# Delta rule in a two-layer trunk: the 32x32 blocks of all chunks inverted by one substitution on VectorE, operands kept in DRAM, weights split once for both halves

## Chip, cores and metric

One core of a Trainium2 chip runs the whole program. The metric is the device time of one execution in microseconds, given as the median of several runs. The profile is one more execution with the hardware profiler on.

## Reference

A trunk of two layers over 1024 tokens of width 1024, all in float32. Layer 0 mixes tokens with a spatial gate (GMLP) and a gated delta rule; layer 1 with differential attention. Each layer then has an MLP and a gated per-layer embedding. Only the delta rule of layer 0 and what shares its input projection matter here:

```
proj = rms_norm(h) @ w_in                     # 1024 x 3080
u, v, q, k, v', z, beta_logit, a_logit = split(proj)
a_out = gelu(u) * (tril(w_s) @ layer_norm(gelu(v)) + b_s)      # per group, 128 tokens at a time
q, k, v' = silu(causal_conv4(q, k, v'));  q, k normalised per head
g = -exp(a_log) * softplus(a_logit + dt_bias);  beta = sigmoid(beta_logit)
# gated delta rule, 4 heads of 128, chunk by chunk:
gc    = cumsum(g);  decay = exp(gc_i - gc_j), lower triangle
A     = strict_lower((beta * k) @ k^T * decay)
T     = inverse(I + A)                        # unit lower triangular
v_new = T @ (beta * v') - T @ (beta * k * exp(gc)) @ state
o     = (q * exp(gc)) @ state + ((q @ k^T) * decay) @ v_new
state = state * exp(gc_last) + (k * exp(gc_last - gc))^T @ v_new
b_out = rms_norm(o) * silu(z)
h     = h + concat(a_out, b_out) @ w_out
```

The reference uses chunks of 64 tokens; the kernel uses 8 chunks of 128, which gives the same result.

## The kernel before

`trunk` runs `even_mix` (layer 0's mixing), then the MLP, embedding and attention. The sequence is held in two halves of 512 tokens. A float32 product is made from three single-pass matmuls (`mm3`: hi x hi, hi x lo, lo x hi). A weight tile is loaded raw (`Weight.load`), cast to its hi part on ScalarE and its lo part taken on VectorE (`split`, lines 220 and 221). Eight raw pieces and twelve split tiles are held.

In `even_mix` two streams share the engines. The first, called fill, is a generator over all tiles of the input projection followed by the first half of the output product (`mix_first`). One step of it, a unit, is three or six matmuls, one or two rows of an output tile's sum. `pump(n)` advances the fill until n units are issued. Each projection tile is 256 columns wide. In the version before, q, k and v of each half are separate tiles (`proj_qkv(i, hf)`), z is shared by the halves (`proj_z`), and u and v of the gate are again separate by half (`proj_uv(hf)`): 22 tiles, each with four split pieces. A q, k or v tile is followed on VectorE by the convolution (L1203, L1209, L1212), and the gate's parts by a layer norm (`norm_v`), small products (`gate`, pgm) and transposes (`put_a`, `put_b`, pab).

The second stream is the recurrence. Per chunk it has three generators. `prep(c)` makes the two decay matrices from pd (L1359, masked at L1360), k's transposes and lengths (pk, L1368 to L1373), the matrix am of k products (pkk, L1394), and the scaled v, q and q-k products (pv, pq, pkq). `inverse(c)` inverts I + A. It takes the sixteen 32x32 diagonal blocks (4 heads, 4 blocks; L1426), inverts them by doubling in four rounds, each with a masked copy on GpSimd (L1434), 16 small products into py, a copy on ScalarE (L1441), 16 into pz, a subtraction (L1449) and a transpose (L1451) on VectorE, and then joins blocks to 64 and to 128 with four more products. Each small float32 product shows as two instructions in the profile. `step(c)` advances the state (pks, po, pvn, pst), and `emit_out` normalises the chunk's output.

The order of issue is written out by hand. A chunk has 12 slots; `chunk` says which generator advances in which slot (`FRONT`), and `FILLS` how many units of fill are issued in it. The recurrence is issued at high priority (`EARLY`). A fill matmul may not come before the recurrence's last matmul of `LAG` = 3 slots earlier (`Ordered`). All instructions go through a scheduler that orders them by a simulated time line before the program is built.

Tiles named by a tag (`slot("c6", ...)`) have one place for each tag; a new tile with the tag waits for the old one's readers.

Of the kernel before, what the change touches and what calls it, by code (L numbers as in the profile page):

```python
# [29 lines left out]
FRONT = (5, 6, 8, 9, 11)  # L30
# [4 lines left out]
FILL0 = (9, 10, 7, 10)  # L35
FILLS = ((0, 2, 1, 4, 5, 4, 0, 1, 3, 1, 4, 1), (0, 3, 2, 3, 1, 5, 3, 1, 4, 0, 3, 0), (0, 6, 2, 2, 2, 3, 0, 1, 3, 0, 3, 2), (0, 5, 3, 5, 4, 6, 1, 2, 5, 1, 4, 2), (0, 7, 5, 4, 0, 8, 0, 0, 7, 0, 3, 3), (1, 6, 3, 3, 5, 2, 1, 2, 5, 2, 3, 1), (1, 5, 0, 3, 2, 4, 3, 2, 4, 1, 5, 6), (0, 3, 5, 6, 6, 3, 4, 3, 3, 2, 4, 1), (1, 0, 1, 1, 0, 4, 0, 1, 0, 2, 3, 0))
# [77 lines left out]
class Trunk:  # L114
# [969 lines left out]
    def even_mix(self, first, rows_of_rest, rest_of_x, w_in, ws, bs, conv, a_log, dt_bias, v_gain, o_gain, masks, w_out, gain_next, h_dram):  # L1084
# [90 lines left out]
        qkv = {}  # L1175

        def proj_qkv(i, hf):
            return [proj_qkv_tile(i, hf, j) for j in range(2)]

        def proj_qkv_tile(i, hf, j):  # L1180
            def units(w):
                if j == 0:
                    qkv[i, hf] = self.slot(f"A{i + 3 * hf}", [P, G, HT], F32, "qkv")

                first = (i, hf, j) == (1, 0, 0)
                pss = [self.mm_ps() for _ in range(2)] if first else []
                for k, ml in itertools.product(range(KT), range(2)) if first else ():
                    self.mm3(pss[ml], w.at(k, slice(ml * P, (ml + 1) * P)), hs_first[k], k == 0, k == KT - 1)
                    if k < KT - 1:
                        yield None  # L1190
                for ml in range(2):
                    m = i * 4 + j * 2 + ml
                    ps = pss[ml] if first else self.mm_ps()
                    for k in range(0 if first else KT):
                        self.mm3(ps, w.at(k, slice(ml * P, (ml + 1) * P)), hs[hf][k], k == 0, k == KT - 1)
                        if k < KT - 1:
                            yield None
                    cx = self.slot(f"c{10 + m % 2}", [P, 3 + HT], F32, "cx")
                    if hf:
                        nc.vector.tensor_copy(cx[:, 0:3], tails[:, m])  # L1200
                    else:
                        nc.vector.memset(cx[:, 0:3], 0.0)
                    nc.vector.tensor_tensor(cx[:, 3:], ps, rb[hf], ALU.mult)  # L1203
                    if not hf:
                        nc.vector.tensor_copy(tails[:, m], cx[:, HT : HT + 3])
                    y = self.tmp()
                    nc.scalar.activation(y, cx[:, 3:], AF.Copy, scale=conv[:, 3, m : m + 1])
                    for tap in range(3):
                        nc.vector.scalar_tensor_tensor(y, cx[:, tap : tap + HT], conv[:, tap, m : m + 1], y, ALU.mult, ALU.add)  # L1209
                    th = self.tmp()  # L1210
                    nc.scalar.activation(th, y, AF.Tanh, scale=0.5)
                    nc.vector.scalar_tensor_tensor(qkv[i, hf][:, m % 4], th, 1.0, y, ALU.add, ALU.mult)  # L1212
                    yield None

            c0 = 1024 + i * 512 + j * 256
            return Proj(f"qkv{hf}", [(w_in[:, c0 : c0 + 256], 0)], 256, units, 16, qkv_lo)


# [16 lines left out]
        def proj_z(j):  # L1235
            def units(w):
                for t2 in range(4):
# [12 lines left out]
                    yield from proj_tok("z", w, t2, done)  # L1250

# [5 lines left out]
        def proj_uv(hf):  # L1257
            g = {}

            def tile_(col, j):  # L1260
                def units(w):
                    if j == 0:
                        g[col] = self.slot((("A1", "A2"), ("A2", "A0"))[col > 0][hf], [P, 4, 512], F32, "guv")
                    for t2 in range(2):
                        def done(ps):
                            for i in range(2):
                                nc.scalar.activation(g[col][:, 2 * t2 + i, j * 256 : (j + 1) * 256], ps[i], AF.Gelu_apprx_tanh, scale=rt(4 * hf + 2 * t2 + i))
                            if j == 1:
                                if col:
                                    norm_v(t2)  # L1270
                                else:
                                    gate(t2)

                        yield from proj_tok(f"uv{hf}", w, 2 * hf + t2, done)
                    if j == 1 and col == 0:
                        yield from put_a()
                        if hf == 0:
                            yield from put_b(0)

                c0 = col + j * 256  # L1280
                return Proj(f"uv{hf}", [(w_in[:, c0 : c0 + 256], 0)], 256, units, 16, uv_lo)

            def norm_v(t2):
                gv = g[512]
                if t2 == 0:
                    g["vg"] = self.slot("c10", [P, 512], F32, "vg")
                    nc.sync.dma_start(g["vg"], v_gain.partition_broadcast(P))
# [14 lines left out]
                for i in range(2):  # L1302
                    t = 2 * t2 + i
                    x = gv[:, t].rearrange("p (g d) -> p g d", d=HD)
                    nc.vector.tensor_tensor(x, x, bc(rv[:, 4 * i : 4 * i + 4], HD), ALU.mult)
                    nc.gpsimd.tensor_tensor(gv[:, t], gv[:, t], g["vg"], ALU.mult)

            def gate(t2):
                gv, gu = g[512], g[0]
                for t in (2 * t2, 2 * t2 + 1):  # L1310
                    ps = aux([P, G, HD], "aux", "pgm")
                    for i in range(G):
                        self.pe.matmul(ps[:, i], lhsT=wT[:, i], rhs=gv[:, t, i * HD : (i + 1) * HD], start=True, stop=True)
                    for i in range(G):
                        a = gu[:, t, i * HD : (i + 1) * HD]
                        nc.vector.scalar_tensor_tensor(a, ps[:, i], bs[:, i : i + 1], a, ALU.add, ALU.mult)

            def put_a():
                for i in range(G):
                    pt = aux([P, 4, P], "tr", "pab")  # L1320
                    for t in range(4):
                        self.pe.transpose(pt[:, t], g[0][:, t, i * HD : (i + 1) * HD], self.ident)
                    put_ab(hf, i, pt)
                    yield

            return [tile_(col, j) for col in (512, 0) for j in range(2)]
# [8 lines left out]
        def put_b(hf):  # L1335
            assert not hf or not outs
            for i in range(G):
                pt = aux([P, 4, P], "tr", "pab")
# [6 lines left out]
        ch = {}  # L1345

        def prep(c):
            hf, cs = c // 4, slice((c % 4) * P, (c % 4 + 1) * P)


# [5 lines left out]
            for own, other in ((gsum, 1), (nsum, -1)):  # L1356
# [5 lines left out]
                yield  # L1362
            dl, du = out
            q, k, v = (qkv[i, hf][:, :, cs] for i in range(3))

            def inverse_length(pt, name):
                sq = self.slot(f"c{4 + c % 2}", [P, G, HD], F32, "sq")
                nc.scalar.activation(sq, pt, AF.Square)  # L1368
                l2 = self.sp.tile([P, G], F32, tag="l2", name=self.nm("l2"))
                nc.vector.tensor_reduce(l2, sq, AX.X, ALU.add)  # L1370
                nc.vector.tensor_scalar(l2, l2, 4 * EPS, None, ALU.add)
                rn = self.sp.tile([P, G], F32, tag=name, name=self.nm(name), bufs=3)
                nc.gpsimd.tensor_tensor(rn, l2, self.mhalf[:, 0:G], ALU.pow)  # L1373
                return rn
# [5 lines left out]
            nc.vector.tensor_tensor(kt, pt, bc(dec[:, c], HD), ALU.mult)  # L1380
            rk = inverse_length(pt, "rk")

            sc = self.sp.tile([P, 3, G], F32, tag="sc", name=self.nm("sc"), bufs=3)
            nc.vector.tensor_tensor(sc[:, 0], rk, rk, ALU.mult)
            nc.vector.tensor_tensor(sc[:, 0], sc[:, 0], beta[:, c], ALU.mult)
            nc.vector.scalar_tensor_tensor(sc[:, 1], sc[:, 0], -1.0, ec[:, c], ALU.mult, ALU.mult)
# [217 lines left out]
        def chunk(st, inv, front, n):  # L1604
            for i in range(12):
                if i in (0, 2, 4):
                    run(st)
# [153 lines left out]
```

## Time and profile before

| | before |
|---|---|
| median of 3 runs | 2600.97 us (2600.1 to 2601.56) |
| profiled execution | 2601.79 us, its span 2600.1 us |
| instructions | 45173 |
| TensorE clock, mean | 0.999 |
| HBM read, written | 277.60 MB, 93.85 MB |
| VectorE busy | 1856.7 us |

`even_mix` takes about the first 500 us of the span: the first projection matmul starts at 10 us, the recurrence's first products at about 84 us, and the last chunk's product po at 452 us. The busy columns of the profile are unions of intervals. The matmul ends are modelled, so a group's mean of one instruction is longer than the distance from one to the next. In a group line the part after the bar is busy time and the mean of one in ns; after the second bar stands the engine's idle time just before these instructions, and what ended it.

### The profile page before, as it was taken

What the parts mean: (1) busy time and instruction counts of PE and PEld (TensorE: products, weight loads), DVE (VectorE), ACT (ScalarE), POOL (GpSimd) and SP (SyncE); (2) the same over time, 40 slices, a digit from 0 to 9 for tenths busy, and PEclk for the clock granted to TensorE, in tenths of its full rate; (3) what the DMA queues carried; (4) which work ended last, traced back from release to release, by engine and by line L of the source; (5) the groups of instructions that cost most, each with busy time, mean ns of one, the idle gap of its engine ahead of it and who ended that gap; (6) DMA issues with size and microseconds to landing.
All of it is one profiled execution on the core that took longest, in us unless ns stands there. A gap on an engine that the chain in (4) does not pass through costs nothing.

```text
span 2600.1 us, 45173 instructions
## 1 busy us (share of the span) xinstructions
PE 2571.4 (99%) x16606; PEld 2212.6 (85%) x16606; DVE 1856.7 (71%) x3736; ACT 1282.0 (49%) x2528; POOL 301.6 (12%) x288
## 2 busy tenths in 40 slices
PE   9999999999999999999999999999999999999999
PEld 7878989888888887888899999988778888888899
DVE  7788667678767779656567777786887677787542
ACT  6543443455445444444446666655654555445421
POOL 0212423000000000000234334310000000000000
PEclk9999999999999999999999999999999999999999
DMA  7322222536555865553311111136466558655511
GB/s 245 86 54 55 75 62 92 166 126 226 196 177 185 282 206 186 188 181 118 109 41 60 42 42 58 62 114 228 167 217 206 170 184 282 207 185 192 185 58 45
DMA packets 281237, 374.42 MB, mean 144 GB/s; under 512 B 25300, under 2 KB 163256, under 8 KB 281016
## 3 DMA queue, kind: packets, MB, share of 16 engines
q1 hardware_dynamic: 280568, 371.47, 43.8%
q8 instruction: 130, 2.13, 0.3%
q14 instruction: 91, 0.75, 0.1%
q10 hardware_dynamic: 448, 0.07, 0.0%
HBM read 277.60 MB, written 93.85 MB: 143 GB/s over the span
## 4 chain that ended last, share of the span: by engine, by line
PE 94%; DVE 3%; ACT 1%; issue 1%; DMA 0%; POOL 0%; ACTq 0%; DVEq 0%; POOLq 0%
PE mm L75 80%; PE po L75 3%; PE qk L75 2%; PE aux L75 2%; PE tr L78 2%; PE py L75 1%; PE pz L75 1%; DVE w L221 1%; PE aux L78 0%; PE pks L75 0%; PE pgm L75 0%; PE pab L78 0%; DMA carved<-in_gdn_out_gain_dram 0%; PE pkq L75 0%; PE pkk L75 0%
## 5 line engine op out<-in xcount | busy, mean ns | idle before, releaser
L220 ACT CAST w<-raw 128x512 fp32r<-128x512 f32 x618 | 378.6, 617 | 476.3 <-PE mm L75 416.6
L75 PE MATMUL mm<-g,w 128*128 128x512 f32 x2592 | 603.2, 394 | 1.0 <-ACT w L220 0.6
L75 PEld LDWEIGHTS mm<-g,w 128*128 128x128 f32 x2592 | 486.3, 188 | 116.0 <-ACT w L220 1.0
L75 PE MATMUL mm<-hi,w 128*128 128x512 f32 x1728 | 559.6, 398 | 0.3 <-ACT hi L1075 0.3
L75 PE MATMUL mm<-w,hi 128*128 128x256 f32 (+1 forms) x2816 | 535.0, 286 | 0.0
L221 DVE TENSOR_TENSOR w<-raw,w 128x512 fp32r<-128x512 f32 (+2 forms) x554 | 384.2, 700 | 185.6 <-ACT w L220 175.1
L75 PEld LDWEIGHTS mm<-w,hi 128*128 128x128 f32 x2816 | 439.3, 189 | 5.3
L75 PE MATMUL mm<-w,lo 128*128 128x256 f32 (+1 forms) x1408 | 398.3, 283 | 0.0
L75 PEld LDWEIGHTS mm<-hi,w 128*128 128x128 f32 x1728 | 325.0, 189 | 75.1 <-ACT hi L1075 0.7
L75 PE MATMUL mm<-lo,w 128*128 128x512 f32 x864 | 341.4, 395 | 1.6 <-DVE lo L1076 0.9
L75 PE MATMUL mm<-t,w 128*128 128x512 f32 x1152 | 270.5, 394 | 1.2 <-ACT w L220 1.2
L75 PEld LDWEIGHTS mm<-w,lo 128*128 128x128 f32 x1408 | 265.9, 189 | 0.6
L75 PEld LDWEIGHTS mm<-t,w 128*128 128x128 f32 x1152 | 216.4, 188 | 52.2 <-ACT w L220 1.6
L75 PEld LDWEIGHTS mm<-lo,w 128*128 128x128 f32 x864 | 162.9, 189 | 37.9 <-DVE lo L229 1.4
L221 DVE TENSOR_TENSOR g<-graw,g 128x512 fp32r<-128x512 f32 x216 | 146.9, 684 | 8.2 <-DMA gd<-g 7.7
L220 ACT CAST g<-graw 128x512 fp32r<-128x512 f32 x216 | 132.6, 617 | 27.6 <-PE mm L75 10.5
L876 ACT ACTIVATE lg<-lg,nm 128x128 f32<-128x128 f32 (+7 forms) x128 | 99.4, 777 | 83.2 <-DVE nm L873 77.0
L257 POOL TENSOR_TENSOR r<-ms,mhalf 128x4 f32<-128x4 f32 x12 | 12.9, 1072 | 1046.9 <-DVE ms L255 1018.7
L347 ACT ACTIVATE g<-g 128x512 f32<-128x512 f32 x96 | 60.5, 631 | 111.6 <-DVE g L281 107.7
L873 DVE CUSTOM_DVE_ANT_0 lg<-qk,al 128x512 f32<-128x512 f32 (+3 forms) x128 | 75.0, 589 | 35.1 <-PE qk L75 31.4
L221 POOL TENSOR_TENSOR w<-raw,w 128x512 fp32r<-128x512 f32 x64 | 84.4, 1343 | 112.0 <-ACT w L220 63.0
L75 PE MATMUL mm<-ohi,w 128*128 128x512 f32 x256 | 85.1, 399 | 0.5 <-ACT ohi L930 0.5
(318 smaller groups left out, 3684.6 us busy)
## 6 DMA issues: line engine op xcount, KB each, us to landing
raw<-in_w_mlp_dram SPq DMA_DIRECT2D x352, 256.0 KB, 3.1
graw<-gd SPq DMA_DIRECT2D x224, 256.0 KB, 2.8
gd<-g SPq DMA_DIRECT2D x192, 256.0 KB, 3.1
raw<-in_w_in_e_dram SPq DMA_DIRECT2D x88, 256.0 KB, 3.1
acc<-h_dram SPq DMA_DIRECT2D x64, 256.0 KB, 4.2
keep<-in_w_mlp_dram SPq DMA_DIRECT2D x64, 256.0 KB, 4.6
h_dram<-acc SPq DMA_DIRECT2D x48, 256.0 KB, 2.8
raw<-in_w_ple_gate_dram SPq DMA_DIRECT2D x48, 256.0 KB, 2.8
```

What stands on the lines that cost most here:

```text
L75: self._next(self.engine.matmul(*a, **k))
L78: self._next(self.engine.transpose(*a, **k))
L220: self.nc.scalar.copy(hi, src)
L221: (lo_engine or self.nc.vector).tensor_tensor(lo, src, f32(hi), ALU.subtract)
L257: nc.gpsimd.tensor_tensor(r, ms, self.mhalf[:, 0:4], ALU.pow)
L347: nc.scalar.activation(g, src, AF.Relu)
L873: nc.vector.tensor_tensor_reduce(out=lg[:, k0:k1], in0=ps[:, : k1 - k0], in1=al[:, u0 + k0 : u0 + k1], scale=-1.0, scalar=3.0e38 if c == 0 ...
L876: nc.scalar.activation(lg[:, :n], lg[:, :n], AF.Exp, bias=nm[:, r, nch - 1 : nch], scale=-1.0, accum_out=me.sums[:, b, r : r + 1])
```

## The change

The diagonal blocks are no longer inverted chunk by chunk. A new generator `ahead(c)` does, for all eight chunks in a row, the part of `prep` that depends on k and the gates only, and stores three tiles of each chunk in DRAM (`spill`: am, the decay for q-k, the scaled transposed k) and the 16 diagonal blocks, one after the other (`diag`). When all eight are stored, `solve` loads the 128 blocks with one block in each partition (32x32 numbers along it) and runs a forward substitution over the columns on VectorE, 30 steps of two instructions. The result goes to DRAM (`solved`). `inverse(c)` then fetches its 16 inverted blocks and am, transposes once, and joins blocks to 64 and 128 as before. `prep(c)` fetches the two other tiles and does v and q.

The scalings of kt, vb and the output o are four 128-wide ScalarE instructions each, one for each head, in place of one VectorE instruction over 512.

The projection tiles are put in another order, and seven more than z are used for both halves: 9 tiles of q, k, v in place of 12, and 4 for the gate in place of 8, so 15 in all. gelu(u) and gelu(v) go to DRAM (`uv_dram`) and come back for the norm and the gates, which run beside the last projection and beside the first half's output product. Slots are now 7 a chunk with the fill shared out evenly (`share`), 40 units over the ahead stage, 64 over the substitution, 48 before the first step, then 24 or 28 a chunk.

```diff
-FRONT = (5, 6, 8, 9, 11)
-FILL0 = (9, 10, 7, 10)
-FILLS = ((0, 2, 1, 4, 5, 4, 0, 1, 3, 1, 4, 1), ...
+FILLA, FILLB, FILLC = 40, 64, 48
+FILLS = (24, 24, 24, 24, 28, 28, 28, 28)
...
+        def keep(c, i, t):
+            nc.sync.dma_start(spill[c, i], flat(t))
+        def fetch(c, i, t):
+            nc.sync.dma_start(flat(t), spill[c, i])
+            return t
+        def ahead(c):
...
+            am, du = out
+            keep(c, 1, du)
+            k = part(1, c)
             pt = aux([P, G, P], "tr", "pk")
...
+            rk = inverse_length(pt, "rk", self.slot(f"c{4 + c % 2}", [P, G, HD], F32, "sq"))
             kt = self.slot(f"c{c % 2}", [P, G, HD], F32, "kt")
-            nc.vector.tensor_tensor(kt, pt, bc(dec[:, c], HD), ALU.mult)
+            for h in range(G):
+                nc.scalar.activation(kt[:, h], pt[:, h], AF.Copy, scale=dec[:, c, h : h + 1])
+            keep(c, 2, kt)
...
             for h in range(G):
-                nc.vector.scalar_tensor_tensor(am[:, h], pp[:, h], sc[:, 0, h : h + 1], dl[:, h], ALU.mult, ALU.mult)
+                nc.vector.scalar_tensor_tensor(am[:, h], pp[:, h], sc[:, h : h + 1], am[:, h], ALU.mult, ALU.mult)
+            for b in range(4):
+                z = slice(32 * b, 32 * b + 32)
+                nc.sync.dma_start(diag[c, :, b].rearrange("h i j -> i h j"), am[z, :, z])
+            keep(c, 0, am)
             yield
+        def solve():
+            work = self.slot("A3", [P, 2, 32, 32], F32, "work")
+            a, x = work[:, 0], work[:, 1]
+            for y in (x, a):
+                nc.sync.dma_start(flat(y), diag.rearrange("c h b i j -> (c h b) (i j)"))
+            nc.vector.memset(flat(x)[:, 0 : 1024 : 33], 1.0)
+            t = self.slot("B", [P, 256], F32, "outer")
+            for j in range(1, 31):
+                n = 31 - j
+                o = t[:, 0 : n * j].rearrange("p (i n) -> p i n", n=j)
+                nc.vector.tensor_tensor(o, a[:, j + 1 :, j : j + 1].to_broadcast([P, n, j]), x[:, j : j + 1, 0:j].to_broadcast([P, n, j]), ALU.mult)
+                nc.vector.tensor_tensor(x[:, j + 1 :, 0:j], x[:, j + 1 :, 0:j], o, ALU.add)
+                if j % 3 == 0:
+                    yield
+            nc.sync.dma_start(solved, flat(x))
...
         def inverse(c):
-            am = mid[c][4]
+            am = fetch(c, 0, self.slot(("c6", "d0")[c % 2], [P, G, P], F32, "am"))
             inv = self.slot("B", [P, 8, G, 32], F32, "inv")
+            xs = inv[:, 0]
+            src = solved[16 * c : 16 * c + 16].rearrange("(h b) (i j) -> b i h j", h=G, j=32)
...
+            for b in range(4):
+                z = slice(32 * b, 32 * b + 32)
+                nc.sync.dma_start(xs[z], src[b])
+                if b < 2:
+                    nc.sync.dma_start(x64[z, :, z], src[b])
+            xst = inv[:, 1]
+            nc.vector.transpose(flat(xst), flat(xs))
...
-            for lv in range(4):
-                m = inv[:, 1]
-                nc.gpsimd.tensor_tensor(m, ad, bc(lm[:, lv], G, 1), ALU.mult)
-                py = aux([P, G, 32], "tr", "py")
-                for h in range(G):
-                    for b in range(4):
-                        z = slice(32 * b, 32 * b + 32)
-                        self.pe.matmul(py[z, h], lhsT=m[z, h], rhs=xst[z, h], start=True, stop=True)
-                yt = inv[:, 6]
-                nc.scalar.copy(yt, py)
-                yield
-                pz = aux([P, G, 32], "tr", "pz")
...
-                nc.vector.tensor_tensor(xst2, xst, pz, ALU.subtract)
-                xs = inv[:, 3 - lv % 2]
-                nc.vector.transpose(flat(xs), flat(xst2))
-                xst = xst2
-                yield
...
+        fill = itertools.chain(self.stream([
+            proj_qkv(1, 0, (0,)), proj_qkv(2, 0, (0,)), proj_qkv(1, 1, (0, 1)), proj_z(0),
+            proj_qkv(1, 0, (1,)), proj_qkv(2, 1, (0, 1)),
+            proj_uv(1, 0), proj_uv(1, 1), proj_qkv(0, 0, (0,)), proj_qkv(0, 1, (0, 1)),
+            proj_z(1), proj_qkv(0, 0, (1,)), proj_qkv(2, 0, (1,)), proj_uv(0, 0), proj_uv(0, 1)], first), mixing())
...
+        SLOTS = ("s", "ip", "s", "i", "p", "si", "ip")
...
+        systems = [ahead(c) for c in range(NC)]
+        for i, n in enumerate(share(FILLA, NC + 1)):
+            if i < NC:
+                run(systems[i], False)
+            if i:
+                run(systems[i - 1], False)
+            self.pe.slot()
+            pump(done + n)
+        for n in share(FILLB, 10):
+            run(solver, False)
+            self.pe.slot()
+            pump(done + n)
+        run(solver, False)
+        self.wide = ("mm",)
+        invs = [inverse(c) for c in range(NC)] + [none]
+        run(invs[0], False)
         f0 = prep(0)
...
+        chunk(none, invs[0], f0, FILLC, ("ip", "i", "i", "i", ""))
+        chunk(none, none, f0, 0, ("p", "p"))
         for c in range(NC):
-            chunk(step(c, states[c]), inverse(c + 1) if c + 1 < NC else none, prep(c + 2) if c + 2 < NC else none, FILLS[c + 1])
-            if c > 2:
+            run(invs[c + 1], False)
+            chunk(step(c, states[c]), invs[c + 1], prep(c + 1) if c + 1 < NC else none, FILLS[c])
+            if "z1" in made:
                 out()
```

In the new order of the fill, counted in units: k of half 0 begins at 0, v at 16, the other k tile for both halves at 32, z at 64, k's first tile for half 1 at 96, v's second tile at 112, the gate's v at 144, q at 208, z's second tile at 256, the rest of q and v at 288, the gate's u at 320, and the output product's first half at 384, with seven units of gates ahead of it. The ahead stage begins at unit 104.

More of the change, by code (lines that the diff above doesn't have):

```diff
@@ L1172, in even_mix, with proj_qkv @@
         qkv_lo, z_lo, uv_lo = nc.vector, nc.vector, nc.vector
[L1175 to L1180, printed above, removed]
+        qkv, made = {}, set()
+        def proj_qkv(i, j, hfs):
             def units(w):
[L1182 to L1195, printed above, removed]
+                for hf in hfs:
+                    if (i, hf) not in qkv:
+                        qkv[i, hf] = self.slot(f"A{i + 3 * hf}", [P, G, HT], F32, "qkv")
+                    first = (i, hf, j) == (1, 0, 0)
+                    pss = [self.mm_ps() for _ in range(2)] if first else []
+                    for k, ml in itertools.product(range(KT), range(2)) if first else ():
+                        self.mm3(pss[ml], w.at(k, slice(ml * P, (ml + 1) * P)), hs_first[k], k == 0, k == KT - 1)
@@ L1206, in units @@
[L1206 to L1212, printed above, removed]
@@ L1250, in units @@
                     yield from proj_tok("z", w, t2, done)
+                made.add(f"z{j}")
             srcs = [(w_in[:, 2560 + j * 256 : 2816 + j * 256], 0)] + ([(w_in[:, 3072:3080], 256)] if j == 0 else [])
             return Proj("z", srcs, 264 if j == 0 else 256, units, 32, z_lo)
[L1257 to L1287, printed above, removed]
@@ new lines, in even_mix, with beside, proj_uv, units @@
+        uv_dram = self.dp.tile([2, NT, P, 512], F32, name="uv_dram")
+        def beside(main, side, every):
+            for n, x in enumerate(main):
+                if n % every == 0:
+                    next(side, None)
+                yield x
+        def proj_uv(col, j):
+            def units(w):
+                for t2 in range(4):
+                    def done(ps):
+                        t = self.tmp()
+                        for i in range(2):
+                            nc.scalar.activation(t[:, 256 * i : 256 * (i + 1)], ps[i], AF.Gelu_apprx_tanh, scale=rt(2 * t2 + i))
+                        nc.sync.dma_start(uv_dram[col, 2 * t2 : 2 * t2 + 2, :, j * 256 : (j + 1) * 256].rearrange("t p f -> p t f"), t.rearrange("p (t f) -> p t f", t=2))
+                    yield from proj_tok("uv", w, t2, done)
+            def last(w):
+                yield from beside(units(w), first_gates(), 3)
+            c0 = col * 512 + j * 256
+            return Proj("uv", [(w_in[:, c0 : c0 + 256], 0)], 256, last if (col, j) == (0, 1) else units, 32, uv_lo)
@@ L1328, in put_ab, with first_gates, second_gates @@
+        def first_gates():
+            norm_v(0)
+            yield from put_b(0)
+            yield from gate(0, (0, 1))
+        def second_gates():
+            norm_v(1)
+            yield from gate(1, range(G))
         def put_ab(hf, k, pt):
@@ L1342, in put_b, with part, inverse_length @@
                 yield
-        ch = {}
-        def prep(c):
-            hf, cs = c // 4, slice((c % 4) * P, (c % 4 + 1) * P)
+        spill = self.dp.tile([NC, 3, P, G * P], F32, name="spill")
+        diag = self.dp.tile([NC, G, 4, 32, 32], F32, name="diag")
+        solved = self.dp.tile([P, 1024], F32, name="solved")
+        nbe = small["nbe"]
+        def part(i, c):
+            hf = c // 4
+            assert all((i, hf, m) in made for m in range(G))
+            return qkv[i, hf][:, :, slice((c % 4) * P, (c % 4 + 1) * P)]
+        def inverse_length(pt, name, sq):
+            nc.scalar.activation(sq, pt, AF.Square)
+            l2 = self.sp.tile([P, G], F32, tag="l2", name=self.nm("l2"))
+            nc.vector.tensor_reduce(l2, sq, AX.X, ALU.add)
+            nc.vector.tensor_scalar(l2, l2, 4 * EPS, None, ALU.add)
+            rn = self.sp.tile([P, G], F32, tag=name, name=self.nm(name), bufs=3)
+            nc.gpsimd.tensor_tensor(rn, l2, self.mhalf[:, 0:G], ALU.pow)
+            return rn
+        def keep(c, i, t):
[4 more added lines that the diff above has]
+        def ahead(c):
             out = []
@@ L1399, in prep @@
             vb = v
[L1400 to L1401 removed]
+            for h in range(G):
+                nc.scalar.activation(vb[:, h], pt[:, h], AF.Copy, scale=hb[:, c, h : h + 1])
             yield
+            q = part(0, c)
             pt = aux([P, G, P], "tr", "pq")
```

211 lines of the change are left out of this document (104 added, 107 removed).

## Prediction

> **What bounds the kernel now.** I read the page first: busy shares, then the chain that ended last.
>
> ```profile
> span 2600.1 us, 45173 instructions
> ...
> PE 2571.4 (99%) x16606; PEld 2212.6 (85%) x16606; DVE 1856.7 (71%) x3736; ACT 1282.0 (49%) x2528; POOL 301.6 (12%) x288
> ...
> PE 94%; DVE 3%; ACT 1%; issue 1%; DMA 0%; POOL 0%; ACTq 0%; DVEq 0%; POOLq 0%
> ```
>
> TensorE is busy for all but 29 us and is 94% of the chain. The time is therefore TensorE's work plus its gaps: only matmuls that go away, or gaps that come or go, can move it. VectorE, ScalarE and DMA count where they make a gap. The busy time by stretches shows where the gaps of the mixing layer lie.
>
> ```profile
> 100.00:140.00 40.00, 40.00 (x437) 31.88 (x436) 36.91 (x86) 19.71 (x45) 8.40 (x12) 1.00 0.30 80
> 140.00:240.00 100.00, 95.04 (x1245) 75.90 (x1243) 86.85 (x230) 40.31 (x90) 21.93 (x31) 1.00 0.19 49
> 360.00:380.00 20.00, 16.17 (x255) 14.63 (x254) 10.12 (x24) 8.56 (x21) 4.58 (x7) 0.83 0.20 68
> 380.00:500.00 120.00, 118.47 (x1113) 105.44 (x1112) 77.26 (x172) 45.59 (x87) 24.74 (x22) 1.00 0.35 112
> ```
>
> The columns after the length are TensorE, its weight loads, VectorE, ScalarE and GpSimd, then TensorE's clock. The gaps sum to 5.0 + 3.8 + 1.5, some 10 us. From 360 to 380 the clock averaged 0.83: 0.17 x 20 = 3.4 us lost besides. Looked at in steps of 2 us, that stretch has one gap and its consequence.
>
> ```profile
> 364.00:366.00 2.00, 0.00 (x0) 0.00 (x0) 1.72 (x3) 0.52 (x2) 1.18 (x3) 1.00 0.01 4
> 368.00:370.00 2.00, 1.54 (x8) 1.14 (x6) 0.97 (x3) 1.01 (x2) 0.00 (x0) 0.50 0.00 0
> ```
>
> So a gap of under 3 us here was followed by half clock, and cost about as much again.
>
> **What is removed from TensorE.** The old inversion runs 4 rounds per chunk, each with one batch of 32 small instructions into py and one into pz: 8 x 4 x 2 = 64 batches. All of them go. The block steps after the rounds, the transposes and the gate products keep their numbers. TensorE's groups by shape for the first 600 us, and a piece of its timeline:
>
> ```profile
> L75 PE MATMUL pz<-inv 32*32 32x32 f32 x1216 | 18.6, 194 | 1.8 <-ACT inv L1441 1.8
> ...
> L75 PE MATMUL py<-inv 32*32 32x32 f32 x1024 | 14.9, 195 | 4.0 <-DVE alo L1332 2.8 <-DVE inv L1449 0.9
> ...
> L75 PE MATMUL pkk<-qkv 128*128 128x128 f32 x64 | 8.7, 279 | 1.1 <-DVE dec L1412 1.1
> ```
>
> ```profile
> 204.53 0.40 PE L75 MATMUL mm<-hi,w 128*128 128x512 f32 x1
> 204.86 0.45 PE L75 MATMUL py<-inv 32*32 32x32 f32 x32
> 205.24 0.50 PE L75 MATMUL mm<-hi,w 128*128 128x512 f32 x1
> 205.58 0.39 PE L75 MATMUL mm<-lo,w 128*128 128x512 f32 x1
> 205.81 0.63 PE L75 MATMUL mm<-hi,w 128*128 128x512 f32 x2
> 206.28 0.40 PE L75 MATMUL mm<-lo,w 128*128 128x512 f32 x1
> ```
>
> From the first hi of a pair to the next lo takes 206.28 - 205.81 = 0.47 us undisturbed, and 205.58 - 204.53 = 1.05 us with a batch in between: alone, a batch costs 0.58 us. Beside another small product it costs 0.38 us in the chain (first row below), and the group's own mean is 14.9 / 32 = 0.47. I take 0.50, between the ends and nearest the mean: 64 x 0.50 = **32 us less work**, 24 to 37 by the ends.
>
> ```profile
> 197.02 0.38 PE py L75 x32
> ```
> ```profile
> 464.12 27.73 PE mm L75 x120
> ```
>
> The waits in the py and pz rows above belong to removed instructions: 4.0 + 1.8 = 5.8 us, the 2.8 us gap among them, and with it 3.4 us of clock. That is **9 us less waiting**, if nothing else is late at those places; 0 if it is.
>
> **What is added.** One unit of fill is three wide matmuls (or six half as wide), 3 x 27.73 / 120 = 0.69 us by the last row. VectorE, ScalarE and GpSimd prices, from the groups by shape between 100 and 445 us, and the two DMA prices:
>
> ```profile
> L221 DVE TENSOR_TENSOR w<-raw,w 128x512 fp32r<-128x512 f32 x67 | 51.2, 776 | 4.8 <-ACT w L220 4.7
> L1209 DVE SCALAR_TENSOR_TENSOR t<-cx,cols,t 128x512 f32<-128x512 f32 x46 | 34.4, 748 | 1.7 <-ACT t L1207 1.2
> ...
> L1370 DVE TENSOR_REDUCE l<-sq 128x4 f32<-128x512 f32 x16 | 10.9, 684 | 6.6 <-ACT sq L1368 6.4
> L1203 DVE TENSOR_TENSOR cx<-mm,rb 128x512 f32<-128x512 f32 x15 | 10.3, 684 | 3.9 <-PE mm L75 3.7
> ...
> L1449 DVE TENSOR_TENSOR inv<-inv,pz 128x128 f32<-128x128 f32 x32 | 9.0, 281 | 16.2 <-PE pz L75 16.2
> L1394 DVE SCALAR_TENSOR_TENSOR dec<-pkk,sc,dec 128x128 f32<-128x128 f32 x32 | 9.0, 342 | 0.0
> ...
> L1371 DVE TENSOR_SCALAR l<-l 128x4 f32<-128x4 f32 x16 | 5.2, 322 | 0.3
> ```
> ```profile
> L1359 ACT ACTIVATE dec<-pd,carved 128x128 f32<-128x128 f32 x64 | 17.9, 374 | 11.7 <-PE pd L75 8.9 <-PE po L75 2.8
> ...
> L1368 ACT ACTIVATE sq<-pk 128x512 f32<-128x512 f32 x8 | 4.8, 597 | 0.6 <-DVE kt L1380 0.5
> ```
> ```profile
> L1373 POOL TENSOR_TENSOR rk<-l,mhalf 128x4 f32<-128x4 f32 x8 | 8.8, 1102 | 68.1 <-DVE l L1371 56.9 <-DVE carved L1205 11.2
> ```
> ```profile
> L673 SPq DMA_DIRECT2D h_dram<-xt x16: 320/339/417, 14.3 to 60.4; - x16
> ```
> ```profile
> raw<-in_w_in_e_dram SPq DMA_DIRECT2D x4, 8.0 KB, 3.9
> ```
>
> *The substitution.* Thirty steps of two VectorE instructions; step j works on j(31 - j) numbers a partition, 4960 in all, so 60 instructions over 9920. By L1449 (128 wide, 0.281) and L1203 (512 wide, 0.684) an instruction is 0.147 us plus 1.05 ns a number: 8.8 + 10.4 = 19 us. Four DMA hops stand around it (blocks out, blocks in, solution out, solution in). The nearest row moves pieces of 32 bytes in 3.9 us; the new ones are 128 bytes: 16 us. Beside it the fill is the u and v projection, whose only large VectorE work is 16 weight splits, 16 x 0.776 = 12 us. Together 47 us. The cover is 64 units of FILLB and, since fill may run three slots past the recurrence, 29 units of FILLC: 93 x 0.69 = 64 us. Hidden, by 17 us; uncovered it would cost 47.
>
> [...] No piece of 128 bytes is in this trace; the 32-byte row above already carries what small pieces cost here.
>
> *The ahead stage* is units 96 to 144, with eight chunks' decay, k lengths and products crowded into it. TensorE: 48 x 0.69 = 33, and 20 instructions of 128x128 per chunk at 8.7 / 64 = 0.136, 8 x 2.7 = 22: 55 us, 6.9 a chunk. VectorE: six conv tiles at 2 x 0.684 + 3 x 0.748 = 3.6, 22; eight splits, 6; per chunk 0.684 + 4 x 0.342 and six tiny ones at 0.32 at most, 4.0, so 32: 60 us. It is as full as TensorE. ScalarE's part, twelve 128-wide pieces at 17.9 / 64 = 0.28 and a square of 0.6 per chunk, is 32 us. The am tile has two places, and each is free only when its five stores have landed. One turn: pd 1.1, eight exponentials 2.2, square 0.6, reduce 0.7, add 0.3, pow 1.1, two tiny 0.6, four products 1.4, five issues on SP's queue at 0.34, landing 3.9: 13.6 us for two chunks, 6.8 each, level with TensorE. But VectorE was 92% busy from 100 to 140, so an arriving instruction nearly always finds another running: with one of 0.7 at each of eight hops the turn is 19.2, 9.6 a chunk. Excess 2.7 x 8 = 22, less the lead of three slots, 3 x 4.4 x 0.69 = 9: **12 us of new gaps**. Bounds 0 (no queueing) and 35 (two queued at each hop).
>
> *Hidden edits.* Twenty-two projections become 15: 28 splits fewer, at 0.776 on VectorE, which no TensorE wait names; nothing gained. The kt, vb and output scalings move to ScalarE, which had half its time free. Some 150 more DMAs of 0.34 on SP are 51 us over some 350. A store waiting on its tile holds the weight loads queued behind it, but eight raw pieces are held, two projections of 11 us or more. Half 1's x must be ready at unit 48 instead of 80; its emission ends at unit 45, so I put that at 0, at most 3. In the later chunks fill is 24 x 0.69 = 17 us plus some 8 of recurrence, 25 a chunk; the inverse's remaining chain is seven issues 2.4, landing 3.9 and about 5 of steps, hidden twice over.
>
> The sum against the profiled execution, which took 2601.8 us, its span and 1.7 around it: 2601.8 - 32 - 9 + 12 = 2572.8. That execution lies 0.8 above the median: **2572 us**.
>
> **Rivals.** *The ahead stage turns slower than TensorE can cover.* With two instructions queued per hop the turn is 24.8 us, 12.4 a chunk: 8 x 5.5 - 9 = 35 us of gaps, in six pieces of over 5 us, each with 3.4 us of half clock, 20 more: 2601.8 - 41 + 55 = 2616, slower. It costs the whole gain from about 10.7 us a chunk (8 x 3.8 - 9 + 20 = 41). For it: 92% busy. Against: the recurrence has priority in its engine's order. Its clock part rests on the row at 0.50: gaps of 5 us are longer than that one, while the forecast's 12 us, in eight pieces of 1.5, are shorter. [...]
>
> *VectorE bounds the last part.* Units 352 to 456 now carry four chunks, both halves' normalisation and gates, and the first output product. From 380 to 500 VectorE had 77 us; two more chunks add 8 x 0.342 + 5 x 0.684 + 6 x 0.32 and 2 of inverse, 20 together, and the first half's normalisation, gates and splits 20 x 0.684 + 16 x 0.342 + 4 x 0.32 = 20: 117 in 120. If sharing with GpSimd stretches it as it did the splits (776 against 684, 13%), 15 us of gaps: 2588.
>
> *The batches ran in time that would stay.* Gaps of the same size open where they were, since the recurrence and not TensorE set the pace; then nothing changes: 2601. The 0.58 of the timeline, in a stream without gaps, speaks against it.
>
> **Chances.** Forecast 0.55; VectorE at the end 0.13, also faster; no change 0.07; the slow ahead stage 0.25. A measurement tells 0.2%, 5 us, from no change. Faster 0.68, same 0.07, slower 0.25. The range starts where work falls by 37, waits by 9 and no gap is new, 2601 - 46 = 2555. It ends at 2612, inside the slow case, of which it leaves out the upper half. The forecast's own range is 2555 to 2590.
>
> **What would show it.** No py or pz of the rounds; TensorE's work down some 32 us; DRAM pieces stored by chunk; the 60 substitution instructions near 19 us. Gaps in the ahead stage of 5 to 20 us prove that step; over 35, or a clock under 0.9 there, the rival. A gap before the first inverse would show that the substitution was not covered. VectorE over 95% in the last part with waits on its splits or sums would be the second rival. Gaps elsewhere of more than 20 us would make the account itself wrong.

## The result and the profile after

The changed kernel takes 2569.14 us in the median (2567.01 to 2571.76), beside 2601.2 for the kernel before. The ratio is 0.9878, with a 95% interval of 0.9861 to 0.9895: 32 us faster. 2572 was predicted. The profiled execution has a span of 2567.1 us, 33.0 less. Its page, in the lines that answer to those shown of before:

```profile
span 2567.1 us, 41117 instructions
...
PE 2540.4 (99%) x14558; PEld 2189.5 (85%) x14558; DVE 1809.8 (70%) x3617; ACT 1274.3 (50%) x2560; POOL 286.3 (11%) x256
...
PE 94%; DVE 3%; DMA 1%; ACT 1%; issue 1%; POOL 0%; SPq 0%; DVEq 0%; ACTq 0%; POOLq 0%
```

TensorE executes 2048 instructions fewer, the 64 batches of 32, and is busy 2571.4 - 2540.4 = 31.0 us less. Its idle time went from 28.7 us to 26.7. These two make the 33.0. Half clock lengthens the busy time too: in the trace of before three fill matmuls of 256 columns took 0.64 us (373.17 to 373.81) at a granted clock of 0.50, and 0.36 us (376.71 to 377.07) at 1.00. By the clock column, an estimate from its averages, 3.4 us were lost to it before and 1.6 after (below), so the work itself fell by some 29. The busy time by stretches shows where the mixing layer now waits; the columns are those of the prediction.

```profile
100.00:140.00 40.00, 37.24 (x230) 32.46 (x229) 32.50 (x91) 30.76 (x98) 18.54 (x22) 1.00 0.53 165
...
360.00:400.00 40.00, 37.88 (x339) 33.27 (x338) 32.16 (x80) 16.67 (x38) 16.44 (x13) 1.00 0.52 163
400.00:440.00 40.00, 38.62 (x215) 33.43 (x215) 26.70 (x58) 13.18 (x25) 5.38 (x5) 0.96 0.47 155
```

The ahead stage (first row) has 2.8 us of gaps, 1.7 of them in one wait ahead of its first product, and the part where the gates and the first output product run (360 to 440) has 3.5 us, with 0.04 x 40 = 1.6 us of clock behind them. Of the waits on the rounds nothing is left. The groups of TensorE with waits or with another price than before:

```profile
L74 PE MATMUL mm<-alo,w 128*128 128x512 f32 x128 | 51.8, 405 | 2.0 <-DVE alo L1350 2.0
...
L77 PE MATMUL pv<-ident,qkv 128*128 128x128 f32 x32 | 10.0, 324 | 0.0
L74 PE MATMUL py<-inv,am 32*32 32x32 f32 x128 | 9.9, 199 | 0.2 <-PE mm L74 0.2
...
L74 PE MATMUL pkk<-qkv 128*128 128x128 f32 x64 | 8.9, 282 | 2.8 <-ACT dec L1400 2.8
```

The same groups of transposes pv and joining products py, in the same number, were cheaper before:

```profile
L78 PE MATMUL pv<-ident,qkv 128*128 128x128 f32 x32 | 5.5, 279 | 0.0
L75 PE MATMUL py<-inv,dec 32*32 32x32 f32 x128 | 5.2, 195 | 1.5 <-DVE inv L1449 1.5
```

The chain of the changed kernel shows why: they now alternate, one transpose after every two instructions of py (one small float32 product). The columns are start and length.

```profile
256.73 0.18 PE py L74 x4
256.91 0.26 PE pv L77
257.17 0.17 PE py L74 x2
257.35 0.26 PE pv L77
257.61 0.17 PE py L74 x2
```

This block of 16 instructions of py and 4 transposes takes 1.98 us in the chain. Before, 16 such instructions with 4 transposes (pk) between them in one piece stood in 1.13 us of the timeline (212.85 to 213.98):

```profile
212.85 0.24 PE L75 MATMUL py<-inv,dec 32*32 32x32 f32 x2
213.02 0.66 PE L78 MATMUL pk<-ident,qkv 128*128 128x128 f32 x4
213.61 0.43 PE L75 MATMUL py<-inv,dec 32*32 32x32 f32 x14
213.98 0.50 PE L75 MATMUL mm<-hi,w 128*128 128x512 f32 x1
```

Something in the change costs TensorE time that the prediction has no step for.

### The profile page after: what moved, and what is told of

Its sections match the earlier page's. It is cut to its first block, busy times and chain, and to the rows that moved or that the text cites. A ratio compares the mean times of both kernels' runs of the same rounds, so it can differ in the third digit from the quotient of the medians.

```text
span 2567.1 us, 41117 instructions
## 1 busy us (share of the span) xinstructions
PE 2540.4 (99%) x14558; PEld 2189.5 (85%) x14558; DVE 1809.8 (70%) x3617; ACT 1274.3 (50%) x2560; POOL 286.3 (11%) x256
## 3 DMA queue, kind: packets, MB, share of 16 engines
HBM read 282.58 MB, written 105.38 MB: 151 GB/s over the span
## 4 chain that ended last, share of the span: by engine, by line
PE 94%; DVE 3%; DMA 1%; ACT 1%; issue 1%; POOL 0%; SPq 0%; DVEq 0%; ACTq 0%; POOLq 0%
PE mm L74 81%; PE po L74 3%; PE qk L74 2%; PE aux L74 2%; PE tr L77 2%; PE aux L77 0%; PE py L74 0%; DVE lg L872 0%; PE pks L74 0%; PE pv L77 0%; PE pkq L74 0%; PE pz L74 0%; DMA carved<-in_gdn_out_gain_dram 0%; DVE lg L883 0%; PE pvn L74 0%
## 5 line engine op out<-in xcount | busy, mean ns | idle before, releaser
L219 ACT CAST w<-raw 128x512 fp32r<-128x512 f32 x590 | 361.3, 618 | 453.2 <-PE mm L74 391.7
L74 PE MATMUL mm<-hi,w 128*128 128x512 f32 x1728 | 552.9, 396 | 0.3 <-ACT hi L1074 0.3
L220 DVE TENSOR_TENSOR w<-raw,w 128x512 fp32r<-128x512 f32 x526 | 360.5, 691 | 188.5 <-ACT w L219 183.4
```

Source lines behind the costliest of these rows:

```text
L74: self._next(self.engine.matmul(*a, **k))
L219: self.nc.scalar.copy(hi, src)
L220: (lo_engine or self.nc.vector).tensor_tensor(lo, src, f32(hi), ALU.subtract)
```

## The experiments

Each kernel was compared with the kernel before on the same chip; a ratio x 2601.2 is the time that stands beside 2569.

**The batches put back.** In `inverse` of the changed kernel:

```diff
+            def rounds():
+                for _ in range(2):
+                    pd2 = aux([P, G, 32], "tr", "pdum")
+                    for h in range(G):
+                        for b in range(4):
+                            z = slice(32 * b, 32 * b + 32)
+                            self.pe.matmul(pd2[z, h], lhsT=xs[z, h], rhs=xst[z, h], start=True, stop=True)
+            rounds()
...
```

The call stands ahead of each of the four groups of products that join blocks.

> The changed kernel with the 64 batches of 32 small products issued again on TensorE (8 in each chunk's inverse, 2 ahead of each of its four products), their results read by nobody; no VectorE, ScalarE or GpSimd work comes back. Theory (the gain is TensorE's work that went away): 64 x 0.50 = 32 us more, 2569 + 32 = 2601; 2593 to 2606 by the ends 0.38 and 0.58. Rival (the gain comes from a freer VectorE and ScalarE and from the waits that went): at most 10 us more, 2569 to 2579.

Measured: ratio 0.9978 (0.9969 to 0.9987), 26 us more than the changed kernel.

```profile
PE 2567.1 (99%) x16606; PEld 2212.2 (85%) x16606; DVE 1808.4 (70%) x3617; ACT 1275.7 (49%) x2560; POOL 287.2 (11%) x256
```

TensorE is busy 26.7 us longer, 0.42 a batch, while VectorE has the changed kernel's 1808. The rival is out: the freer VectorE does not make the gain, the batches do. The 0.42 is not the price of one batch, though. The batches also part py from pv, whose groups are back near their prices of before, and longer gaps in the output product lost 0.16 x 40 = 6.4 us of clock, beside 1.6:

```profile
L77 PE MATMUL pv<-ident,qkv 128*128 128x128 f32 x32 | 5.1, 276 | 0.0
L74 PE MATMUL py<-inv,am 32*32 32x32 f32 x128 | 4.4, 198 | 0.0
```
```profile
400.00:440.00 40.00, 36.45 (x457) 31.15 (x455) 24.41 (x58) 13.73 (x31) 12.86 (x9) 0.84 0.35 113
```

**The rounds left out of the kernel before.**

```diff
             for lv in range(4):
-                m = inv[:, 1]
...
                 yield
...
                 yield
```

Everything in the four rounds but the two `yield` goes.

> The kernel before with the four rounds left out (so the 32x32 blocks are not inverted, only I minus the first level), everything else in place: hand-written slots, separate projections, no DRAM store. Theory (TensorE's work plus the waits on the rounds): 2601 - 32 - 6 - 3 = 2560, 2557 to 2577. Rival (the recurrence sets the pace and the gaps open elsewhere): 2596 to 2601. Second rival (the gain needs the shared splits and the new order): 2585 or more.

Measured: ratio 0.9832 (0.9818 to 0.9847), 2558, 44 us less than before.

```profile
PE 2533.3 (99%) x14558; PEld 2188.3 (86%) x14558; DVE 1830.9 (72%) x3672; ACT 1268.9 (50%) x2494; POOL 287.5 (11%) x256
```

TensorE's busy time falls by 38.1 us, 0.60 a batch, near the 0.58 of the prediction's timeline for a batch alone in the fill. In the timeline of before only 32 of the 64 stand between two fill matmuls; why the others cost no less is not shown. So the rounds alone were worth 44 us, and the changed kernel keeps only 32 of it. Neither rival holds.

**py ahead of pv.** The search for the other 12 began with the alternation.

```diff
-                for g in what:
-                    run(gens[g], False)
+                for n, g in enumerate(what):
+                    self.pe.floor = self.pe.mark if n else None
+                    run(gens[g], False)
+                    self.pe.floor = None
```

> The changed kernel with an order of issue between two generators that advance in one slot: the transposes pv come after the last product py of that slot, where the trace of the changed kernel has them alternating, 1.98 us in its chain for what took 1.13 apart. Theory (each change between a 32-row product and a transpose costs TensorE): 7 chunks x 0.9 = 6 us less, 2563; 2561 to 2566. Rival (only the ends are modelled so, the alternation is free): 2567 to 2571.

Measured: ratio 0.986 (0.9846 to 0.9875), 4.7 us less than the changed kernel by the ratios; the intervals overlap. The trace is clearer than the times:

```profile
PE 2534.1 (99%) x14558; PEld 2188.0 (85%) x14558; DVE 1809.4 (71%) x3617; ACT 1276.2 (50%) x2560; POOL 287.0 (11%) x256
```
```profile
L77 PE MATMUL pv<-ident,qkv 128*128 128x128 f32 x32 | 5.4, 286 | 0.4 <-DVE qkv L1210 0.4
...
L74 PE MATMUL py<-inv,am 32*32 32x32 f32 x128 | 3.5, 194 | 0.0
```

Busy time falls by 6.3 us. With that the account of TensorE's busy time closes: 2571.4 - 38.1 + 6.3 = 2539.6, beside 2540.4 measured. The alternation itself may cost more than 6.3: the row below has 0.13 x 40 = 5.2 us of lost clock, beside 1.6, and up to 3.6 us of that lengthen this run's busy time. Part of the gain went into a larger gap at the start of the output product:

```profile
360.00:400.00 40.00, 34.18 (x256) 29.70 (x256) 30.53 (x74) 14.11 (x31) 17.34 (x14) 0.87 0.45 149
```

**Late heads first.** On top of that, the order of summing in `mix_out` for half 0:

```diff
+        ks = [*range(4, n), *range(4)] if h == 0 and n == KT else [*range(n)]
...
-            for k in range(n):
+            for k in ks:
...
```

> The last kernel, and the first output product of half 0 sums its delta-rule heads (k = 4 to 7) ahead of the gate's (k = 0 to 3), whose last two are made just before. In the changed kernel that product waited 2.0 us for them, beside 0.5 on the gate, and the clock then lost 1.7. Theory: those gaps close, 3.5 us less than the last kernel, 2559.5. Rival (the gap moves to the other four heads): no difference to the last kernel, within 1.5.

Measured: ratio 0.9822 (0.9808 to 0.9837), 2555 us, 14 us faster than the changed kernel and 10 faster than the last one, against 3.5 expected.

```profile
360.00:400.00 40.00, 38.16 (x293) 33.62 (x292) 35.00 (x88) 16.93 (x36) 19.68 (x14) 0.96 0.53 172
```

Against the row above, 4.0 us of gaps and 0.09 x 40 = 3.6 us of clock closed, 7.6 of the 10. Most of these gaps and of this clock had come with the order of py and pv. This is the fastest version of the study.

**No alternation anywhere in the recurrence.** The same with every group's matmuls held behind the group issued before it, in `run`; this takes the place of the edit that put py ahead of pv:

```diff
+        marked = [None]
...
+            was = self.pe.mark
+            self.pe.floor = marked[-1]
             with self.tc.high_priority(EARLY):
                 end = next(g, 1)
+            self.pe.floor = None
+            if self.pe.mark != was:
+                marked.append(self.pe.mark)
```

> The kernel with late heads and py before pv, and now every group of the recurrence's products behind the last product of the group issued before it, so that no two groups of the recurrence can alternate on TensorE; the fill is free as before. Theory (a change between small products and transposes or wider products costs 0.25 us or more of TensorE): the groups that still alternate (pkq with po, pk with pd) fall into blocks, 2 to 4 us less, 0.980 to 0.982 of the kernel before. Rival (a fixed order makes groups wait for one another and gaps open): 0.983 to 0.990.

Measured: ratio 0.9823 (0.9808 to 0.9837), no difference. Busy time was 2530.3, 2.7 more than without the hold. The theory fails here: between groups of products 128 wide nothing was won.

**No priority.** `EARLY = 0` in the changed kernel.

> The changed kernel with EARLY = 0, so the recurrence, the ahead stage and the substitution are issued in program order with the fill and not ahead of it. The prediction put an instruction of 0.7 us ahead of the ahead stage at each of eight hops, a turn of 9.6 us a chunk, and 12 us of gaps; 2.8 were measured. Theory (it is the priority that keeps the hops short): without it the turn goes to 9 us or more and the ahead stage has 12 us of gaps or more, 2580 to 2640 in all. Rival (the hops are short anyway, since VectorE was less full than taken): 2567 to 2575.

Measured: ratio 0.9987 (0.9977 to 0.9998), 28 us slower than the changed kernel, but not by the mechanism expected. The ahead stage kept its gaps (1.4 us from 100 to 140) and nearly its pace (5.8 us a chunk, beside 5.5 below). The loss is TensorE's busy time, 2573.3 us beside 2540.4: the small products now alternate with the fill. Some 8 us of it are half clock (the mean clock is 0.996, beside 0.999).

```profile
L74 PE MATMUL pz<-inv 32*32 32x32 f32 x192 | 12.9, 201 | 0.0
```
```profile
366.44 0.24 PE L74 MATMUL pz<-inv 32*32 32x32 f32 x2
366.61 0.39 PE L74 MATMUL mm<-w,hi 128*128 128x256 f32 x1
366.93 0.24 PE L74 MATMUL pz<-inv 32*32 32x32 f32 x2
367.10 0.39 PE L74 MATMUL mm<-w,hi 128*128 128x256 f32 x1
```

The group pz is at 12.9 us, beside 3.8 in the changed kernel. One pair of instructions, a single small product, and one fill matmul take 0.49 us here.

**One place for am.** `e = self.slot("c6" if other > 0 else ...)` in `ahead`.

> The changed kernel with one place in place of two for the am tile in the ahead stage, so a chunk's decay waits until the stores of the one before have landed. The prediction's account of the turn without queueing: 13.6 less pd 1.1 and less 2.4 for the landing (1.5 measured, 3.9 taken) is 10.1 us a chunk against 6.9 of TensorE work: 8 x 3.2 - 9 = 17 us of gaps, 2586, to 2600 with clock. With queueing as predicted (0.7 at each of eight hops) 15.7 a chunk: 8 x 8.8 - 9 = 61 us, 2630 and more. Rival (the stage is never bound by the turn): 2567 to 2573.

Measured: ratio 0.9971 (0.9959 to 0.9983), 24 us slower, 2594, in the range of the account without queueing. The products pkk, one group a chunk, show the turn: first the changed kernel's chunks 1 and 7, then this kernel's chunks 0 and 6.

```profile
112.53 1.11 PE L74 MATMUL pkk<-qkv 128*128 128x128 f32 x8
...
145.46 1.05 PE L74 MATMUL pkk<-qkv 128*128 128x128 f32 x8
```
```profile
108.74 1.16 PE L74 MATMUL pkk<-qkv 128*128 128x128 f32 x8 [1.72 <-ACT dec L1400]
...
165.50 1.16 PE L74 MATMUL pkk<-qkv 128*128 128x128 f32 x8 [1.90 <-ACT dec L1400]
```

With one place a turn takes (165.50 - 108.74) / 6 = 9.5 us, where 10.1 were expected unqueued and 15.7 queued. TensorE's waits ahead of pkk sum to 15.2 us in seven pieces, beside the 17 expected. With two places the stage runs at (145.46 - 112.53) / 6 = 5.5 us a chunk.

**The substitution doubled.** Each product three times into the same tile.

> The changed kernel with each product of the substitution done three times into the same tile, so 120 instructions in place of 60, some 22 us more on VectorE between the ahead stage and the first inverse. Theory (covered by 64 us of fill; the chain from the last store to the first product on the solution was 45 us): 45 + 22 = 67, 3 us late and at most 3 us of clock, 2569 to 2576. Rival (no slack): 22 us more and clock, 2591 to 2595.

Measured: ratio 0.9972 (0.9961 to 0.9983), 24 us slower; the rival's figure, by another road.

```profile
L1446 DVE TENSOR_TENSOR outer<-work x90: 190/349/410, 159.8 to 216.9; 128x30 f32<-128x30 f32 x6, 128x58 f32<-128x58 f32 x6, 128x84 f32<-128x84 f32 x6, 128x108 f32<-128x108 f32 x6
L1447 DVE TENSOR_TENSOR work<-work,outer x30: 191/349/408, 160.6 to 217.1; 128x30 f32<-128x30 f32 x2, 128x58 f32<-128x58 f32 x2, 128x84 f32<-128x84 f32 x2, 128x108 f32<-128x108 f32 x2
```
```profile
PE py L74 <- DVE inv L1493: 15.7, 1, 15.7
```

The substitution ended at 217.1, 34 us later than in the changed kernel (183.2), not 22: the later it runs, the more of q's convolution stands on VectorE in between. TensorE stood still from 208.8 to 224.5, in one wait of 15.7 us ahead of the first py. The granted clock averages 0.70 from 200 to 240, and for some 5 us after the wait TensorE ran slower: three wide matmuls took 1.28 us (227.99 to 229.27), and 0.69 us from 230.40 on. In the changed kernel the transposed solution was there at 191.9 and that product came at 196.2. Here TensorE found other work until 208.8, less two waits on q's convolution that sum to 4.2. It could therefore cover some 208.8 - 191.9 - 4.2 = 12.7 us more than it had to. The work is covered, but by a margin of 13 us, and of only 4.3 in the order in which the changed kernel was built.

**Projections split by half again.** `proj_qkv(1, 1, (0,)), proj_qkv(1, 1, (1,))` for `(0, 1)`, and so for the other six; once on the changed kernel, once on the fastest.

> The changed kernel with its seven shared q, k, v, u, v-gate projections split by half again, 22 projections in place of 15, in the same order of work: 28 more weight splits (0.62 us each on ScalarE, 0.72 on VectorE) and 7 MB more of loads. Theory (the sharing is hidden and worth nothing): 2567 to 2573. Rival (the relief of VectorE is part of the gain): 28 x 0.72 = 20 us more, 2580 to 2590.

> The kernel with late heads and py before pv, with the seven shared projections split by half again (22 projections, 28 more splits). The earlier run without sharing was 4 to 5 us slower than the changed kernel, 4.1 us of that in one wait on the gate's heads. Theory (the splits are hidden, and that wait was the fill's order): with that order mended it equals the shared kernel, 0.981 to 0.984 of the kernel before. Rival (VectorE, full in the last part, makes the splits cost): 4 us more or beyond, 0.9838 to 0.990.

Measured: on the changed kernel 0.9895 (0.9878 to 0.9911), 4 us slower with overlapping intervals. On the fastest 0.9854 (0.9838 to 0.9871) beside 0.9822 (0.9808 to 0.9837), 8 us slower. Both theories that the splits are hidden fail, the second clearly. In the trace of the second the stretch from 360 to 400 waits more than in the fastest kernel's row above:

```profile
360.00:400.00 40.00, 35.01 (x259) 30.45 (x259) 29.70 (x73) 14.40 (x32) 15.79 (x13) 0.91 0.54 176
```

That is 3.2 us of gaps and 0.05 x 40 = 2.0 of clock. The two longest waits in it, and what VectorE did ahead of the first:

```profile
366.77 0.69 DVE L1304 TENSOR_REDUCE mean<-guv 128x4 f32<-128x512 f32 x1 [4.41 <-DMA guv<-uv_dram]
368.12 0.68 PE L74 MATMUL pgm<-guv,wT 128*128 128x128 f32 x4 [1.97 <-DVE guv L1333]
391.31 2.08 PE L74 MATMUL pvn<-qkv,xt 128*128 128x128 f32 x8 [2.27 <-DVE qkv L1545]
```

Ahead of the first, VectorE was not full: it stood idle for 4.41 us, waiting for gelu(v) to come back from DRAM, and the gate's product (L1333) stood behind that. Ahead of the second it was busy without a pause (8.00 of 8 us from 384 to 392). The edit also brings back 7 MB of loads (289.92 MB read, beside 282.58) and gives the fetches other places in the DMA queue. So what the shared projections save is shown, but not that VectorE's splits are the reason; the first wait speaks for the transfers.

## Why the prediction was right, point by point

That the time came out 3 us from the forecast is in part luck: the batches were worth 6 us more than reckoned, the alternation took 6 or more back, and 12 us of gaps were forecast where fewer came.

*Work of the batches:* 32 us predicted, 31.0 less busy, 1.8 of them clock. The mechanism is shown from both sides, by leaving the rounds out and by putting batches back. The 0.50 a batch is right only as a sum of two errors. Leaving them out gave 0.60 a batch, the upper end, 38 us; the change gives 6 or more back by alternating py with pv, a term that the prediction lacked. It counted the joining products and the transposes as unchanged because their number was, and a slot that advances two generators changed their order.

*Waits:* 9 us, clock included, were to go and 12 to come. The waits on the rounds went. Those that came were 2.8 in the ahead stage and 3.5 later, with 1.6 of clock. Gaps and clock together fell by about 4 (2.0 of gaps, and 1.8 of clock that is inside the 31.0), where the forecast had them rise by 3. The largest wait that the prediction counted as gone, 2.8 us ahead of py, named `alo`, the lo part of an operand of the output product, and not the rounds. In the changed kernel the output product waits 2.0 us for `alo`, and that is where the clock falls now.

```profile
107.91 1.16 PE L74 MATMUL pkk<-qkv 128*128 128x128 f32 x8 [1.71 <-ACT dec L1400]
401.38 0.80 PE L74 MATMUL mm<-alo,w 128*128 128x512 f32 x1 [1.66 <-DVE alo L1350]
```

The prediction took gaps of 1.5 us to cost no clock, being shorter than the 2.8 of its trace. With the second of these, 1.66 us long after three shorter ones that sum to 1.4 within 8 us, the clock fell to half (0.50 from 402 to 404); after the first, 1.71 us long, it stayed at 1.00. By these rows the length of one gap alone does not tell.

*The ahead stage:* the mis-sized term is the queueing. The forecast was 12 us of gaps, and its own sign for this step was 5 to 20; 2.8 came. Of these 1.7 lie ahead of the first chunk's product, while ScalarE worked without a pause (4.00 of 4 us from 104 to 108). The other 1.05 come from the turn: ScalarE waited 3.4 us there for a store of am to land. The turn was reckoned at 13.6 us unqueued, with 3.9 for a landing that was 1.5 in the trace for the blocks (median of 32 stores) and 2.3 for the larger tiles (median of 16), and 0.7 of waiting was added at each of eight hops. At 5.5 us a chunk, the turn of two chunks took at most 11.0. The run with one place shows 9.5, below even the unqueued 10.1, which leaves no room for the 5.6 us of queueing. Nor is that due to the priority, since the run without it kept the pace. VectorE was busy 32.5 of 40 us there, not 92%.

*The substitution:* 19 us predicted, 10.0 + 9.9 = 19.9 measured:

```profile
L1446 DVE TENSOR_TENSOR work<-work,outer 128x30 f32<-128x30 f32 (+14 forms) x30 | 10.0, 332 | 1.0
L1445 DVE TENSOR_TENSOR outer<-work 128x30 f32<-128x30 f32 (+14 forms) x30 | 9.9, 331 | 3.1 <-DMA work<-diag 2.2
```

The whole chain, from the last store's issue at 151.6 to the transposed solution at 191.9, took 40 us, beside 47. Its four DMA hops landed in 1.5, 5.4, 3.0 and 1.8 us (medians by issue), together 11.7 us where the prediction took 16 from the row of 32-byte pieces. The run with the doubled substitution puts what could cover it at 13 us more, beside 17.

*Hidden edits:* half wrong. Sharing the splits was put at nothing and is worth 4 us here, with overlapping intervals, and 8 in the best order. The step took the absence of waits on splits in the trace of before as proof, though the new order makes the last part denser, on VectorE and in the DMA queue; which of the two costs the time stays open. The rival of a full VectorE was half right: VectorE is full in places of the last part, 4.00 of 4 us from 392 to 396, and the gaps there are small, 3.5 us and not 15 (13% on top of 117 us would pass the 120 by 12). The 13% is a mean of unequal cases: in the trace of before the long splits ran beside GpSimd work (1.58 us at 280.49, 1.19 at 317.56), while others beside it took 0.69 (279.68, 351.96). The SP queue can be held, as the step said: in the trace of before nothing was issued on it from 66.95 to 76.29, until the store of z had its data from GpSimd, and the next load followed at 76.84.

*The rival of gaps that stay* is out by the run without rounds.

## What to carry to other kernels

Where an engine is busy 99% of the time, price a removed instruction by the distance between its neighbours in the timeline, with and without it, and ask for each removed one what stood beside it. Then look at what the new order puts next to each other on that engine: small products that alternate one by one with wide matmuls or transposes cost 6 us or more of a saving of 38 here, and one order constraint brought that back. A term that is added for queueing should be tested where the queue can be made longer by a known amount, as one place for two did here.

## What was not expected of the hardware

A pair of 32-row instructions between wide matmuls costs TensorE far more than its share of a block: 0.49 us with one fill matmul of 0.12 (three took 0.36 just before, 364.56 to 364.92), so some 0.37, beside 0.58 for 32 of them in one piece. And the clock fell with no gap that the profile shows, where they alternated. In the run without priority TensorE was busy without a pause:

```profile
364.00:368.00 4.00, 4.00 (x33) 3.35 (x31) 0.00 (x0) 0.59 (x1) 3.01 (x3) 1.00 0.19 66
368.00:372.00 4.00, 4.00 (x21) 2.58 (x21) 0.00 (x0) 0.00 (x0) 0.00 (x0) 0.71 0.26 66
372.00:376.00 4.00, 4.00 (x19) 3.44 (x19) 1.98 (x5) 1.17 (x2) 0.00 (x0) 0.50 0.00 0
```

The alternation starts at 366.4, and by 372 the granted clock is 0.50. The ends of matmuls are modelled, so this busy share does not show that TensorE was at work all the time. A busy share of 100% is thus no proof of full clock: from 372 to 376 it stands beside 0.50. The clock column has to be read beside it. No run shows why the clock fell there.
